# A decoder layer on one core: sums placed apart from their readers in groups of seven, and four more groups of seven in the second gate/up products

## The chip, the cores and the metric

The kernel runs on one core of one Trainium2 chip. The metric is the device time of one execution in microseconds (us). Three runs of the kernel before took 2227.22, 2227.85 and 2228.51 us; the median is 2227.85 us.

## The reference

One decoder layer over 256 tokens of width 2048, in float32: a half feed-forward, a pair of token mixers, a second half feed-forward and a gated embedding, each followed by a layer norm. The change touches the feed-forwards, above all the second one:

```python
def swiglu(x, w_gu, w_down):
    g, u = jnp.split(x @ w_gu, 2, axis=-1)
    return (jax.nn.silu(g) * u) @ w_down
...
        h = layer_norm(alpha * h + 0.5 * swiglu(h, w_ffn1_gu[i], w_ffn1_down[i]), ln_g[i, 0], ln_b[i, 0])
...
        h = layer_norm(alpha * h + 0.5 * swiglu(h, w_ffn2_gu[i], w_ffn2_down[i]), ln_g[i, 2], ln_b[i, 2])
```

Here `x` is 256 x 2048, `w_gu` 2048 x 11264 (gate and up side by side) and `w_down` 5632 x 2048.

## The kernel before

**Products in three parts.** Every float32 number is held as a high part of the type `fp32r` and a low part, the rest. ScalarE (ACT) makes the high part with a cast, VectorE (DVE) the low part with a subtraction (line 107 and line 108). A product then takes three matmuls on TensorE (PE): low x high, high x high, high x low (lines 459 to 461, the method `add` of `Sum`).

**Blocks and units.** The gate/up products run in eleven blocks `j` of 512 gate and 512 up columns; `f2` in a name is the second feed-forward, `f1` the first. The 2048 rows of the weights are cut into eight pairs `p` of 128-row pieces, and each block handles each pair as one unit. The order of the units is a string of letters, one unit each, in `gu_units`:

- `P`, plain: two weight chunks of 512 KB (gate and up) are loaded, and each is made into high and low: two casts on ACT and two subtractions on DVE of 128x1024. PE does 24 matmuls.
- `F`, folded: as `P`, but the low part of the second chunk is made by ACT (the negated copy, line 170) and an accumulating DMA from the POOL queue (line 171), so that DVE has one subtraction less.
- `S`, a group of seven (class `Seven`): the 2x2 block product of two token halves and two column halves is done with seven products in place of eight, 21 matmuls. It needs sums of the weights first: `t1` and `t3` (tile `uf_gu`, lines 256 and 257), `t2` and `t4` (tile `vf_gu`, lines 258 and 259), all on DVE at 128x512. Then four splits follow, each a cast on ACT and a subtraction on DVE: the first chunk (`hf_gu`, `lf_gu`), the block b22 (`bf_gu`, half the size), and the two sums (`huf_gu`, `luf_gu`; `hvf_gu`, `lvf_gu`).
- `D`, prepared (class `Prepared`): a group of seven whose sums were made and written to DRAM during the mixers; it loads them, and only two splits are left.

A block's groups of seven share four PSUM banks (`f22s` for block 2, `f23s` for block 3) beside the four of its gate and up results (`f2g`, `f2u`).

**What sets the order.** The program is recorded by hand: each engine executes its instructions in the order in which the code issues them. `fill` takes units from `plan`, loads them and makes them (the splits and sums) as far ahead of PE as `room` has slots and as the queue is below 45 us of matmul time. So a make stands in DVE's and ACT's streams among the other work of the block: after a block's last group of seven, `seven_common` (lines 578 to 582) takes the shared banks out; after its last unit, lines 1085 to 1087 add the gate and up banks, apply Silu on ACT and multiply. One to five units later a transposed copy of the result is fetched and put together by ACT (`f2a<-mf`, line 226, two copies).

Of the kernel before, what the change touches and what calls it, by code (L numbers as in the profile page):

```python
# [9 lines left out]
F32R = mybir.dt.float32r  # L10
# [3 lines left out]
ALU = mybir.AluOpType  # L14
PSUM = bass.MemoryType.PSUM

P = 128
# [26 lines left out]
SEVEN = (0, 1, 2, 3)  # L44

AHEAD = {1: (4, 5), 2: (4,), 3: (4, 5), 4: (4,), 5: (4, 5), 6: (4,), 7: (4, 5), 8: (4,)}
AHEAD_SLOTS = 36

DELAY = {"f1": 2, "f2": 1}

# [14 lines left out]
def layer(ctx: ExitStack, tc: tile.TileContext, io):  # L65
    nc = tc.nc
    sync, act, dve, pool, pe = nc.sync, nc.scalar, nc.vector, nc.gpsimd, nc.tensor
# [14 lines left out]
    def slot(shape, dt, name):  # L82
        return slots.tile(shape, dt, tag="slot", name=name)
# [22 lines left out]
    def split(dst_hi, dst_lo, src, lo_engine=None):  # L106
        act.copy(dst_hi, src)  # L107
        (lo_engine or dve).tensor_tensor(dst_lo, src, dst_hi, ALU.subtract)  # L108

    class Chunk:  # L110
# [18 lines left out]
        def make(self):  # L129
            self.make_hi()  # L130
            split(self.hi, self.lo, self.raw)
# [71 lines left out]
    class Turn:  # L203
# [7 lines left out]
        def part(self):  # L211
            of_src = self.src.bitcast(U16).rearrange("p a (n h) -> p h a n", h=2)
            self.words = slot([P, 2, self.a, self.b * P], U16, "w" + self.name)
            for h in range(2):
                act.copy(self.words[:, h], of_src[:, h])
# [17 lines left out]
    class Seven:  # L233
# [12 lines left out]
        def make(self):  # L246
            a, b = self.a, self.b
            nm = a.name
            b11, b21, b12, b22 = a.of(a.raw, 0), a.of(a.raw, 1), b.of(b.raw, 0), b.of(b.raw, 1)
            u, v = (slot([P, 2, 512], F32, w + nm) for w in "uv")  # L250

            def shaped(x):
                return x.rearrange("p (g n) -> p g n", g=2) if a.paired else x

            t1, t3, t2, t4 = (shaped(x) for x in (u[:, 0], u[:, 1], v[:, 0], v[:, 1]))
            dve.tensor_tensor(t1, b11, b12, ALU.add)
            dve.tensor_tensor(t3, b12, b22, ALU.add)  # L257
            dve.tensor_tensor(t2, b11, t3, ALU.add)
            dve.tensor_tensor(t4, t2, b21, ALU.add)  # L259

            def parted(name, x):
                hi, lo = (slot([P, 2, 512], F32R, w + name + nm) for w in "hl")
                split(hi, lo, x)
                return [(hi[:, e], lo[:, e]) for e in range(2)]

            a.make()
            self.b11, self.b21 = a.columns(0), a.columns(1)
            both = slot([P, 2, 512], F32R, "b" + nm)
            self.b22 = both[:, 0], both[:, 1]
            split(shaped(both[:, 0]), shaped(both[:, 1]), b22)  # L270
            self.t1, self.t3 = parted("u", u)
            self.t2, self.t4 = parted("v", v)

    put_by_sums = {}

# [108 lines left out]
    def slots_for_weights(n, ahead=45, far=90):  # L384
        room.update(slots=n, ahead=ahead, far=far)
# [177 lines left out]
    def units_of(order, sevens, ahead=()):  # L563

        sevens, ahead = list(sevens), list(ahead)
        plain = [p for p in range(KD // 2) if p not in sevens + ahead]
        of = {"S": sevens, "D": ahead, "P": plain, "F": plain}
        return [(kind, of[kind].pop(0)) for kind in order]
# [397 lines left out]
    def gu_units(name, j):  # L966
        if j == 0:
            return [("P", p) for p in range(KD // 2)]
        if name == "f2" and j in AHEAD:
            plain = "P" if j < 4 else "F"  # L970
            return units_of(*((f"P{plain}SDSDSP", SEVEN[:3]) if j % 2 else (f"P{plain}SSDSSP", SEVEN)), AHEAD[j])
        order = "FFSSFSSP" if name == "f1" or j > 8 else "PFSSFSSP"
        return units_of(order, SEVEN[: order.count("S")])

# [20 lines left out]
    def plan_ffn(name):  # L995
        for j in range(KF // 4):
            block_units(gu_units(name, j), gu_keys(name, j))
        first, second, held = down_units(HELD_PAIRS[name == "f2"])
        block_units(first, down_keys(name, 0))
        block_units(second, down_keys(name, 1))  # L1000
        plan.extend(Single(down_keys(name, 1)(n, p)) for n in range(2) for p in held)

    def ffn(name, i, ht, norm, keep, residual, keepers, away):
# [33 lines left out]
        for j in range(KF // 4):  # L1037
            pg, pu = banks(f"{name}g{j}"), banks(f"{name}u{j}")
            units = gu_units(name, j)
            n_of = {(0, 0): KD, (0, 1): KD, (1, 0): KD, (1, 1): KD}  # L1040
            for kind, p in units:
# [18 lines left out]
            def before(u, j=j, offset=KD // 2 - len(units)):  # L1060
# [14 lines left out]
                if name == "f2" and j and u == 0:  # L1075
                    slots_for_weights(AHEAD_SLOTS - j)
                if j == KF // 4 - 1 and u in (4, 6):
# [895 lines left out]
```

## Time and profile before

| | |
|---|---|
| median of three runs | 2227.85 us |
| span of the profiled execution | 2226.9 us |
| instructions in it | 29164 |
| granted TensorE clock | 0.999 |
| DVE busy | 2006.5 us, 90% |
| ACT busy | 1440.9 us, 65% |
| POOL busy | 51.7 us, 2% |

The profiled execution has no time of its own beside its span; its span is 0.95 us below the median of the runs, which is what lies around the first and last instruction. The page gives the busy time of each engine, the chain of work that ended last, and the costliest groups of instructions; the trace behind it also gives each instruction with its start, its duration and what the engine waited for. In the second gate/up products, blocks 1 to 10 run from 1492.5 to 1896.2 us, about 40.1 us each.

### The profile page before, as it was taken

To read this page: it belongs to the slowest core of one execution; us is meant where nothing else is said; L and a number is where in the kernel's file an instruction comes from. 1 tells how busy PE (TensorE), PEld (TensorE's weight loads), DVE (VectorE), ACT (ScalarE), POOL (GpSimd) and SP (SyncE) were. 2 spreads that over 40 slices of the span, in tenths; PEclk is the share of its full clock that TensorE was granted. 3 is DMA by queue.
4 is the path that set the end of the run, shared out by engine and by line. 5 is a ranking of instruction groups with operands and counts; after the bars stand their busy time and mean duration, and the time that the engine had idled before them with its cause. 6 is when DMAs were issued, how large, how long until landed. Compare 5 with 4: busy or idle time off the path is not lost.

```text
span 2226.9 us, 29164 instructions
## 1 busy us (share of the span) xinstructions
PE 2216.5 (100%) x10137; PEld 1838.3 (83%) x10137; DVE 2006.5 (90%) x2629; ACT 1440.9 (65%) x1680; POOL 51.7 (2%) x66
## 2 busy tenths in 40 slices
PE   9999999999999999999999999999999999999998
PEld 7888888888888888888788888888888888888887
DVE  6999999999988889789999888779999999999977
ACT  6777777776565545557866567466666677765553
POOL 0000000000000000000000000000000000000000
PEclk9999999999999999999999999999999999999999
DMA  9998998978686889846976568888999988777871
GB/s 310 275 251 251 266 271 233 246 228 256 216 301 239 297 281 336 268 172 228 293 232 236 179 205 319 312 302 270 303 297 298 332 240 270 215 237 240 292 283 68
DMA packets 303917, 576.02 MB, mean 259 GB/s; under 512 B 98829, under 2 KB 103821, under 8 KB 303769
## 3 DMA queue, kind: packets, MB, share of 16 engines
q1 hardware_dynamic: 293576, 541.70, 73.4%
q0 software_dynamic: 8208, 29.89, 7.2%
q10 hardware_dynamic: 1984, 2.58, 0.4%
q8 instruction: 79, 1.29, 0.2%
q14 instruction: 70, 0.57, 0.1%
HBM read 490.20 MB, written 33.55 MB: 235 GB/s over the span
## 4 chain that ended last, share of the span: by engine, by line
PE 94%; DVE 2%; DMA 2%; issue 1%; ACT 0%; SPq 0%; ACTq 0%; DVEq 0%; POOLq 0%
PE f1g L461 3%; PE f1g L459 3%; PE f1g L460 3%; PE rqk L410 3%; PE f1u L461 2%; PE f1u L459 2%; PE f1u L460 2%; PE f2g L461 2%; PE f2g L459 2%; PE f2g L460 2%; PE f2u L461 2%; PE f2u L459 2%; PE f2u L460 2%; PE aqk L410 2%; PE f2e L461 1%; PE f2e L460 1%
## 5 line engine op out<-in xcount | busy, mean ns | idle before, releaser
L108 DVE TENSOR_TENSOR lf_gu<-rf_gu,hf_gu 128x1024 fp32r<-128x1024 f32 (+1 forms) x225 | 268.6, 1210 | 24.9 <-ACT hf_gu L107 24.1
L107 ACT CAST hf_gu<-rf_gu 128x1024 fp32r<-128x1024 f32 (+1 forms) x225 | 229.7, 1039 | 24.7 <-DMA rf_gu<-in_f_gu 24.1
L108 DVE TENSOR_TENSOR lw_in_f<-rw_in_f,hw_in_f 128x1024 fp32r<-128x1024 f32 x140 | 167.9, 1219 | 14.0 <-ACT hw_in_f L107 13.6
L108 DVE TENSOR_TENSOR lf_down<-rf_down,hf_down 128x1024 fp32r<-128x1024 f32 x128 | 153.9, 1220 | 17.3 <-ACT hf_down L107 14.5
L107 ACT CAST hf_down<-rf_down 128x1024 fp32r<-128x1024 f32 x128 | 131.5, 1049 | 41.9 <-DMA rf_down<-in_f_down 15.3
L107 ACT CAST huf_gu<-uf_gu 128x1024 fp32r<-128x1024 f32 x76 | 80.1, 1054 | 113.9 <-DVE uf_gu L257 104.1
L107 ACT CAST hw_in_f<-rw_in_f 128x1024 fp32r<-128x1024 f32 x140 | 140.6, 1048 | 5.9 <-DMA rw_in_f<-in_w_in_f 2.9
L107 ACT CAST hvf_gu<-vf_gu 128x1024 fp32r<-128x1024 f32 x76 | 80.2, 1055 | 32.0 <-DVE vf_gu L259 29.8
L108 DVE TENSOR_TENSOR luf_gu<-uf_gu,huf_gu 128x1024 fp32r<-128x1024 f32 x76 | 92.6, 1218 | 0.0
L108 DVE TENSOR_TENSOR lvf_gu<-vf_gu,hvf_gu 128x1024 fp32r<-128x1024 f32 x76 | 92.6, 1218 | 0.0
L459 PE MATMUL f1g<-hf_gu,xt 128*128 128x512 f32 x232 | 90.6, 390 | 1.5 <-ACT hf_gu L107 1.5
L461 PE MATMUL f1g<-lf_gu,xt 128*128 128x512 f32 x232 | 90.4, 389 | 0.0
L460 PE MATMUL f1g<-hf_gu,xt 128*128 128x512 f32 x232 | 90.3, 389 | 0.0
L459 PE MATMUL f2g<-hf_gu,ht 128*128 128x512 f32 x208 | 81.0, 390 | 0.0
L461 PE MATMUL f2g<-lf_gu,ht 128*128 128x512 f32 x208 | 80.9, 389 | 0.0
L460 PE MATMUL f2g<-hf_gu,ht 128*128 128x512 f32 x208 | 80.9, 389 | 0.0
L459 PE MATMUL f1u<-hf_gu,xt 128*128 128x512 f32 x192 | 74.7, 389 | 0.0
L460 PE MATMUL f1u<-hf_gu,xt 128*128 128x512 f32 x192 | 74.7, 389 | 0.0
L461 PE MATMUL f1u<-lf_gu,xt 128*128 128x512 f32 x192 | 74.7, 389 | 0.0
L171 POOL DMA_DIRECT2D lf_gu<-rf_gu x41 | 35.5, 868 | 1637.7 <-PE f2u L461 989.0
L1086 ACT ACTIVATE eve<-eve 128x1024 f32<-128x1024 f32 x20 | 21.2, 1061 | 74.0 <-DVE eve L1085 74.0
L107 ACT CAST huf_down<-uf_down 128x1024 fp32r<-128x1024 f32 x32 | 33.7, 1052 | 49.7 <-DVE uf_down L257 42.4
(1524 smaller groups left out, 6990.8 us busy)
## 6 DMA issues: line engine op xcount, KB each, us to landing
rf_gu<-in_f_gu SPq DMA_DIRECT2D x362, 512.0 KB
rf_down<-in_f_down SPq DMA_DIRECT2D x176, 512.0 KB
rw_in_f<-in_w_in_f SPq DMA_DIRECT2D x148, 512.0 KB
lf_gu<-rf_gu POOLq DMA_DIRECT2D x41, 512.0 KB, 7.9
rw_rv<-in_w_rv SPq DMA_DIRECT2D x32, 512.0 KB
rw_ret<-in_w_ret SPq DMA_DIRECT2D x32, 512.0 KB
rw_mix<-in_w_mix SPq DMA_DIRECT2D x32, 512.0 KB
rw_pg<-in_w_pg SPq DMA_DIRECT2D x32, 512.0 KB
```

Of the source, the lines that this page charges most:

```text
L107: act.copy(dst_hi, src)
L108: (lo_engine or dve).tensor_tensor(dst_lo, src, dst_hi, ALU.subtract)
L171: pool.dma_start(c.lo, c.raw, accum_op=ALU.add)
L410: pe.matmul(ps[f], hi[:, kk, f * P : (f + 1) * P], rhs(k), start=k == 0, stop=k == n_k - 1,)
L459: pe.matmul(o, al, bh, start=first, stop=False)
L460: pe.matmul(o, ah, bh, start=False, stop=False)
L461: pe.matmul(o, ah, bl, start=False, stop=self.left == 0)
L1086: act.activation(g, g, AF.Silu)
```

## The change

`Seven.make` issues its work in another order, with the same 8 operations on DVE and 4 on ACT, and `gu_units` gives other letters to blocks 3, 5, 7 and 9 of the second feed-forward:

| block | before | after |
|---|---|---|
| 3 | PPSDSDSP | PSDSSDSP |
| 5, 7 | PFSDSDSP | PSDSSDSP |
| 9 | FFSSFSSP | FSSFSSSP |

```diff
+SEVEN_MORE = 4
+FIVE = {"f1": (), "f2": (9,)}
@@ class Seven, make
-            dve.tensor_tensor(t1, b11, b12, ALU.add)
-            dve.tensor_tensor(t3, b12, b22, ALU.add)
-            dve.tensor_tensor(t2, b11, t3, ALU.add)
-            dve.tensor_tensor(t4, t2, b21, ALU.add)
-            def parted(name, x):
-                hi, lo = (slot([P, 2, 512], F32R, w + name + nm) for w in "hl")
-                split(hi, lo, x)
-                return [(hi[:, e], lo[:, e]) for e in range(2)]
-            a.make()
-            self.b11, self.b21 = a.columns(0), a.columns(1)
             both = slot([P, 2, 512], F32R, "b" + nm)
             self.b22 = both[:, 0], both[:, 1]
-            split(shaped(both[:, 0]), shaped(both[:, 1]), b22)
-            self.t1, self.t3 = parted("u", u)
-            self.t2, self.t4 = parted("v", v)
+            def part(name):
+                hi, lo = (slot([P, 2, 512], F32R, w + name + nm) for w in "hl")
+                return hi, lo, [(hi[:, e], lo[:, e]) for e in range(2)]
+            dve.tensor_tensor(t3, b12, b22, ALU.add)
+            dve.tensor_tensor(t1, b11, b12, ALU.add)
+            a.make_hi()
+            self.b11, self.b21 = a.columns(0), a.columns(1)
+            act.copy(a.hi, a.raw)
+            act.copy(shaped(both[:, 0]), b22)
+            dve.tensor_tensor(t2, b11, t3, ALU.add)
+            dve.tensor_tensor(a.lo, a.raw, a.hi, ALU.subtract)
+            dve.tensor_tensor(t4, t2, b21, ALU.add)
+            dve.tensor_tensor(shaped(both[:, 1]), b22, shaped(both[:, 0]), ALU.subtract)
+            uh, ul, (self.t1, self.t3) = part("u")
+            act.copy(uh, u)
+            dve.tensor_tensor(ul, u, uh, ALU.subtract)
+            vh, vl, (self.t2, self.t4) = part("v")
+            act.copy(vh, v)
+            dve.tensor_tensor(vl, v, vh, ALU.subtract)
@@ gu_units
+            if j % 2 and j > 1:
+                return units_of("PSDSSDSP", SEVEN, AHEAD[j])
+        if j in FIVE[name]:
+            return units_of("FSSFSSSP", SEVEN + (SEVEN_MORE,))
```

Where two blocks meet, DVE's stream changes most. These are its rows before, at the end of block 2 and the beginning of block 3 (`f22s`, `f2g` and `f2u` are banks of block 2; `_0_6` is the gate chunk of pair 6, `_0_0` that of pair 0, the first group of seven of block 3):

```order
L582 TENSOR_TENSOR evw<-f22s_13857,eve 128x512
L108 TENSOR_TENSOR lf_gu_0_6_14182<-rf_gu_0_6_14125,hf_gu_0_6_14181 128x1024
L108 TENSOR_TENSOR lf_gu_1_6_14210<-rf_gu_1_6_14127,hf_gu_1_6_14209 128x1024
L1085 TENSOR_TENSOR eve<-eve,f2g_13850 128x512
L1085 TENSOR_TENSOR eve<-eve,f2g_13851 128x512
L1085 TENSOR_TENSOR evw<-evw,f2u_13852 128x512
L1085 TENSOR_TENSOR evw<-evw,f2u_13853 128x512
L1087 TENSOR_TENSOR evw<-eve,evw 128x1024
L256 TENSOR_TENSOR uf_gu_0_0_14239<-rf_gu_0_0_14158,rf_gu_1_0_14160 128x512
L257 TENSOR_TENSOR uf_gu_0_0_14239<-rf_gu_1_0_14160 128x512
L258 TENSOR_TENSOR vf_gu_0_0_14240<-rf_gu_0_0_14158,uf_gu_0_0_14239 128x512
L259 TENSOR_TENSOR vf_gu_0_0_14240<-vf_gu_0_0_14240,rf_gu_0_0_14158 128x512
```

And these are the rows of the change at the same place, from the last read of block 2's shared banks on:

```order
L592 TENSOR_TENSOR evw<-f22s_13857,eve 128x512
L267 TENSOR_TENSOR uf_gu_0_0_14189<-rf_gu_1_0_14127 128x512
L268 TENSOR_TENSOR uf_gu_0_0_14189<-rf_gu_0_0_14125,rf_gu_1_0_14127 128x512
L273 TENSOR_TENSOR vf_gu_0_0_14190<-rf_gu_0_0_14125,uf_gu_0_0_14189 128x512
L274 TENSOR_TENSOR lf_gu_0_0_14195<-rf_gu_0_0_14125,hf_gu_0_0_14194 128x1024
L275 TENSOR_TENSOR vf_gu_0_0_14190<-vf_gu_0_0_14190,rf_gu_0_0_14125 128x512
L276 TENSOR_TENSOR bf_gu_0_0_14191<-rf_gu_1_0_14127,bf_gu_0_0_14191 128x512
L279 TENSOR_TENSOR luf_gu_0_0_14203<-uf_gu_0_0_14189,huf_gu_0_0_14202 128x1024
L282 TENSOR_TENSOR lvf_gu_0_0_14207<-vf_gu_0_0_14190,hvf_gu_0_0_14206 128x1024
L1099 TENSOR_TENSOR eve<-eve,f2g_13850 128x512
L1099 TENSOR_TENSOR eve<-eve,f2g_13851 128x512
L1099 TENSOR_TENSOR evw<-evw,f2u_13852 128x512
```

The first group of seven of block 3 is now made ahead of the reading of block 2's gate and up banks (line 1085 before, 1099 now), where it stood behind it; and in its own make the subtraction `lf_gu` now stands between the two sums of `vf_gu`, where the four sums stood side by side.

On PE, block 3 changes at its second unit. Before, plain pair 3 was followed by plain pair 6 (the first row is the last matmul of pair 3):

```order
L461 MATMUL f2u_14221<-lf_gu_1_3_14155,ht_12969 128x512
L459 MATMUL f2u_14222<-hf_gu_1_3_14154,ht_12969 128x512
L460 MATMUL f2u_14222<-hf_gu_1_3_14154,ht_12969 128x512
L461 MATMUL f2u_14222<-lf_gu_1_3_14155,ht_12969 128x512
L459 MATMUL f2g_14219<-hf_gu_0_6_14181,ht_12969 128x512
```

In the change plain pair 6 comes first and the group of seven of pair 0 right behind it:

```order
L471 MATMUL f2u_14239<-lf_gu_1_6_14155,ht_12969 128x512
L469 MATMUL f23s_14240<-hf_gu_0_0_14194,ht_12969 128x512
L470 MATMUL f23s_14240<-hf_gu_0_0_14194,ht_12969 128x512
L471 MATMUL f23s_14240<-lf_gu_0_0_14195,ht_12969 128x512
L469 MATMUL f2g_14236<-hf_gu_0_0_14194,ht_12969 128x512
```

PE reaches the first group of seven of block 3 one plain unit (24 matmuls) earlier than before. In all, PE has 12 matmuls less, DVE 27 subtractions and additions more, ACT eight casts more and three negated copies less, and POOL three accumulating DMAs less. The loads of weights are the same in number and size.

## The prediction

> **What bounds the kernel now.** I read the page first (busy time, chain), then the waits of the second gate/up stage, then single blocks of it in the windows and the timelines.
>
> ```profile
> PE 2216.5 (100%) x10137; PEld 1838.3 (83%) x10137; DVE 2006.5 (90%) x2629; ACT 1440.9 (65%) x1680; POOL 51.7 (2%) x66
> PE 94%; DVE 2%; DMA 2%; issue 1%; ACT 0%; SPq 0%; ACTq 0%; DVEq 0%; POOLq 0%
> ...
> PE f2u L461 <- DMA lf_gu<-rf_gu: 0.8, 1, 0.8
> ```
>
> PE is busy for nearly the whole span and is the chain. In blocks 1 to 10 of the second gate/up stage (1492.5 to 1896.2 us) it waits once, 0.8 us, for the accumulating DMA of a folded unit. A reader who stops here would credit every matmul removed. But DVE stands right behind PE there:
>
> ```profile
> 1572.70:1612.80 40.10, 40.10 (x178) 33.22 (x177) 37.79 (x46) 27.93 (x31) 0.87 (x1) 1.00 0.85 277
> 1612.80:1652.90 40.10, 40.10 (x178) 33.22 (x177) 39.16 (x48) 26.50 (x30) 0.86 (x1) 1.00 0.94 297
> DVE uf_gu L256 <- DMA rf_gu<-in_f_gu: 4.2, 2, 2.5
> DVE lf_gu L108 <- ACT hf_gu L107: 4.0, 10, 0.5
> DVE evw L1085 <- PE f2u L461: 3.1, 4, 1.4
> DVE evw L579 <- ACT eve L578: 1.7, 2, 1.0
> ```
>
> The windows are blocks 3 and 4 (columns: window, length, then busy of PE, PEld, DVE, ACT, POOL). DVE has 37.8 of 40.1 us in an odd block and 39.2 in an even one. The waits are DVE's in the whole stage: 13.0 us in some 404, of which 3.1 are waits for PE, true spare time. How far DVE is ahead is seen in the last group of seven of block 2:
>
> ```profile
> 1556.60 0.69 DVE L256 TENSOR_TENSOR uf_gu<-rf_gu,rf_gu 128x512 f32<-128x512 f32 x1
> 1557.20 0.68 DVE L257 TENSOR_TENSOR uf_gu<-rf_gu 128x512 f32<-128x512 f32 x1
> 1557.99 0.69 DVE L258 TENSOR_TENSOR vf_gu<-rf_gu,uf_gu 128x512 f32<-128x512 f32 x1
> 1558.71 0.69 DVE L259 TENSOR_TENSOR vf_gu<-vf_gu,rf_gu 128x512 f32<-128x512 f32 x1
> 1559.33 1.22 DVE L108 TENSOR_TENSOR lf_gu<-rf_gu,hf_gu 128x1024 fp32r<-128x1024 f32 x1
> 1560.46 0.68 DVE L108 TENSOR_TENSOR bf_gu<-rf_gu,bf_gu 128x512 fp32r<-128x512 f32 x1
> 1561.06 1.22 DVE L108 TENSOR_TENSOR luf_gu<-uf_gu,huf_gu 128x1024 fp32r<-128x1024 f32 x1
> 1562.20 1.22 DVE L108 TENSOR_TENSOR lvf_gu<-vf_gu,hvf_gu 128x1024 fp32r<-128x1024 f32 x1
> 1563.33 1.22 DVE L108 TENSOR_TENSOR lf_gu<-rf_gu,hf_gu 128x1024 fp32r<-128x1024 f32 x1
> 1564.91 2.36 DVE L108 TENSOR_TENSOR lf_gu<-rf_gu,hf_gu 128x1024 fp32r<-128x1024 f32 x2 [0.35 <-ACT hf_gu L107]
> ...
> 1564.09 0.39 PE L460 MATMUL f22s<-hvf_gu,f2fh 128*128 128x512 f32 x1
> 1564.31 0.39 PE L461 MATMUL f22s<-lvf_gu,f2fh 128*128 128x512 f32 x1
> ```
>
> `lvf_gu` is ready at 1562.20 + 1.22 = 1563.42, PE reads it at 1564.31: a lead of 0.9 us. In this stage PE and DVE are two bounds side by side. What DVE gets more than its spare time and this lead, PE has to wait.
>
> **The change part by part.** *Matmuls.* Four units of 24 become four of 21: 12 matmuls less. One starts 0.22 us (1564.31 - 1564.09; 0.227 over longer rows) behind the other, though each is shown with 0.39. That is 12 x 0.227 = 2.7 us less on PE. It is worth that only where DVE keeps up.
>
> *Sums apart from readers.* From start to start a 128x512 operation takes 0.60 us (1557.20 - 1556.60), but `t4`, which reads `t2`, starts 0.72 behind it (1558.71 - 1557.99), and `t2`, which reads the sum before it, 0.79 here. Other groups show 0.72 for both. So 2 x 0.12 = 0.24 us go for each group of seven once no reader stands right behind its sum.
>
> ```profile
> L256 DVE TENSOR_TENSOR uf_gu<-rf_gu,rf_gu 128x512 f32<-128x512 f32 x36 | 24.6, 685 | 4.2 <-DMA rf_gu<-in_f_gu 4.2
> ```
>
> There are 36 groups in these blocks: 36 x 0.24 = 8.6 us less on DVE. Elsewhere the same saving falls where PE has hardly a wait to lose, and I count it nothing.
> [...]
>
> *Four more groups.* A new group takes DVE 4 x 0.60 for the sums, 0.60 for `bf_gu` and 3 x 1.135 (1561.06 to 1562.20 to 1563.33) for the other low parts: 6.41 us. It takes the place of a plain unit in block 3 (2 x 1.135 = 2.27) and of a folded one in blocks 5, 7 and 9 (1.135 each, the rest of its work is ACT's and a DMA's). That is 25.64 - 2.27 - 3.41 = 20.0 us more on DVE. The left-hand forms of pair 4 exist already for the prepared units, so block 9 needs none. ACT gets some 3 us more of casts, hidden in its 12 us of spare time per block. The loads are the same; three accumulating DMAs go.
>
> *The tail on ACT.* `hvf_gu` needs `t4`. Now `t4` stands behind `lf_gu` on DVE:
>
> ```profile
> 1559.49 1.05 ACT L107 CAST hvf_gu<-vf_gu 128x1024 fp32r<-128x1024 f32 x1 [0.47 <-DVE vf_gu L259]
> 1560.45 1.05 ACT L107 CAST hf_gu<-rf_gu 128x1024 fp32r<-128x1024 f32 x1
> 1561.40 2.57 ACT L226 COPY f2a<-mf 128x1024 uint16<-128x1024 uint16 x2
> 1563.84 2.94 ACT L107 CAST hf_gu<-rf_gu 128x1024 fp32r<-128x1024 f32 x3
> ```
>
> Queued behind `hvf_gu` on ACT are a cast, two copies of 2.57 us together and the cast for which DVE waits at 1564.91 (0.35 us). Before, `t4` ends 1559.40 - 1556.60 = 2.80 us behind the group's start. In the new order it ends at 3 x 0.60 + 1.135 + 0.69 = 3.63. ACT's tail begins 0.83 later, and DVE arrives 0.24 earlier: the wait grows by 1.07 us. The ten waits of 4.0 us above are this one, once a block, so DVE loses 10 x 1.07 = 10.7 us. The bounds are 0, if ACT catches up elsewhere (as it does where no copies stand behind a group), and 10 x 1.5 = 15, if the first groups of a block wait too. I take 10.7: same rows, same places.
>
> *PE's turn at block 3, 5, 7, 9.* The first group now comes after one plain unit, 24 x 0.227 = 5.4 us. Its bank, by the order of the program, was a gate bank of the block before, and the reading of it now stands behind the whole make:
>
> ```profile
> 1568.32 0.68 DVE L579 TENSOR_TENSOR evw<-eve,f22s 128x512 f32<-128x512 f32 x1
> 1571.03 2.35 DVE L108 TENSOR_TENSOR lf_gu<-rf_gu,hf_gu 128x1024 fp32r<-128x1024 f32 x2
> 1573.30 1.28 DVE L1085 TENSOR_TENSOR eve<-eve,f2g 128x512 f32<-128x512 f32 x2
> 1583.58 0.39 PE L459 MATMUL f23s<-hf_gu,ht 128*128 128x512 f32 x1
> ```
>
> Today the bank is read at 1573.30 and written at 1583.58. In the change, DVE is at 1571.03 + 6.41 = 1577.4 when it begins to read, done at 1578.1, and PE arrives at 1583.58 - 5.44 = 1578.1. Nothing is left over: any lag of DVE shows here as a wait of PE. This is a place, not a further price, since DVE does the same work.
>
> *Sum.* DVE: 20.0 - 8.6 + 10.7 = 22.1 us more. Against that stand the waits that it can give up: 3.1 for PE surely, 5.9 for DMA (4.2) and for ACT at line 579 (1.7) perhaps. DMAs come at 277 and 297 GB/s in the two windows, with a share of 0.85 and 0.94, so a slower stage leaves them some room; I count a third, 2. With the lead of 0.9: 22.1 - 3.1 - 2 - 0.9 = **16 us slower**. As DVE bounds these blocks then, the 2.7 us of PE and its one wait are not to be had besides. The profiled span of 2226.9 gets 2243; with the 0.95 us between it and the median, 2227.85 + 16 = 2244 us.
>
> **The rivals.**
> 1. *PE stays the bound.* If DVE's lead did suffice, 2.7 us go, and at most the 0.8 of waiting: 2224.3. For it speaks PE at 100%; against it the 0.9 us of lead and the 20 us that come. It decides if DVE's net gain in work is below its 13 us of waits, that is, if the tail term is nought and all waits can be filled. Chance 0.06.
> 2. *The tail does not grow.* 22.1 - 10.7 - 3.1 - 2 - 0.9 = 5.4: 2233. For it: ACT has 12 us spare a block; against it: its four instructions are in a row without idle time in the view. Chance 0.12.
> 3. *The bubbles stay.* By the rows this needs a hold on DVE at every sum, though no reader is next: 16 + 8.6 = 24.6, so 2252.5. [...] Chance 0.05.
> 4. *More waits.* The folded unit that remains inside block 9 has its DMA landing late already:
>
> ```profile
> 1837.93 0.50 PE L461 MATMUL f2u<-lf_gu,ht 128*128 128x512 f32 x1 [0.78 <-DMA lf_gu<-rf_gu]
> ```
>
> It is issued behind ACT's work for the groups ahead of it; PE now reaches it with no lead, so it may cost some 4 us more, and the DMA waits may all remain (2): 16 + 6 = 22, or 2250. Chance 0.07.
>
> That the change does not do what it says is excluded: the rows of the program show the 12 matmuls gone.
>
> **How the numbers follow.** The forecast, 2244, has 0.70. Its own bounds: without the tail's growth in half the blocks and with all waits filled 16 - 5.4 - 3.9 = 7, with the larger tail and no DMA wait filled 16 + 4.3 + 2 = 22: 2235 to 2250. The range goes from 2232 to 2252, so that it takes in rivals 2 and 4; left out are rivals 1 and 3 and the forecast's edges, under 2 in 10. A measurement of this kernel can tell some 0.2%, 4.5 us, from no change. Faster by that would need more than rival 1 gives: 0.02. Within it: the rest of rival 1 and half of rival 2, 0.10. Slower: 0.88.
>
> **What would show it.** In the changed profile: ten waits of `lf_gu` for `hf_gu` of about 1.4 us in place of 0.4; no waits of line 1085's successor for PE; starts of 0.60 us throughout the sums; PE waiting a microsecond or two at the first `f23s`, `f25s`, `f27s` and `f29s`, and for `luf_gu` or `lvf_gu` in the last groups of the even blocks; the folded unit inside block 9 waiting longer than 0.8; a PE as before outside the stage. I am wrong if PE runs through blocks 1 to 10 without such waits, or if the loss arises outside them.

## The result, and the profile after

Four runs of the changed kernel took 2244.1 to 2248.14 us, median 2245.47; the kernel before took 2227.66 beside them. The ratio is 1.0085, with a 95% interval of 1.0073 to 1.0098: slower by some 18 us (17.8 between the medians, 18.9 by the ratio). The profiled span is 2244.2 us, 17.3 longer than before.

The busy times and the chain of the changed kernel's page:

```profile
PE 2220.9 (99%) x10125; PEld 1836.8 (82%) x10125; DVE 2004.4 (89%) x2656; ACT 1442.8 (64%) x1685; POOL 49.2 (2%) x63
PE 92%; DVE 4%; DMA 2%; ACT 1%; issue 1%; SPq 0%; ACTq 0%; DVEq 0%
```

Read by themselves these lines would hide the change: over the whole span DVE is *less* busy than before. In the second gate/up products its busy time rises from 419.2 to 433.1 us; outside them it falls by 16.0, because sums that start 0.60 us apart overlap in the records, where each is shown with some 0.69. What is new is DVE's share of the chain, 4% in place of 2, at PE's cost. The loss is all in the second gate/up products: from 1446.0 to 1913.6 us after, from 1447.0 to 1896.2 before, 18.4 us more. They begin 1.0 us earlier, but that is not shown to be the change's: in e2 and e6, experiments below that keep the old order of the sums, they begin at 1445.7 and 1444.7 us.

The waits of PE in these products (what waited, for what, us in total, times, longest), where before there was one row of 0.8 us:

```profile
PE f2u L471 <- DMA lf_gu<-rf_gu: 6.2, 3, 4.7
PE f27s L469 <- DVE eve L1099: 1.8, 1, 1.8
PE f25s L469 <- DVE eve L1099: 1.8, 1, 1.8
PE f23s L469 <- DVE eve L1099: 1.5, 1, 1.5
PE f29s L469 <- DVE eve L1099: 1.2, 1, 1.2
PE f28s L471 <- DVE luf_gu L279: 0.8, 1, 0.8
PE f26s L471 <- DVE luf_gu L279: 0.7, 1, 0.7
PE f29s L471 <- DVE lf_gu L274: 0.5, 1, 0.5
```

PE waits for DVE at the first group of seven of blocks 3, 5, 7 and 9, in the last groups of the even blocks, and for the folded units in blocks 9 and 10. DVE's own waits in the same stretch:

```profile
DVE lf_gu L112 <- ACT hf_gu L111: 17.0, 11, 2.1
DVE evw L589 <- ACT eve L588: 1.9, 2, 1.0
DVE f2f2l L112 <- ACT f2f2h L111: 1.2, 1, 1.2
DVE lf_gu L274 <- ACT hf_gu L271: 1.1, 1, 1.1
DVE evw L1099 <- PE f2u L471: 0.9, 1, 0.9
```

The waits for DMA (4.2 us before) are gone, those for PE are 0.9 instead of 3.1, and the waits of `lf_gu` for `hf_gu` are 17.0 us instead of 4.0. DVE has become the later of the two engines, and ACT keeps it waiting once a block.

How one late block end runs on into the next block is seen in the timeline between blocks 4 and 5. First DVE (start, duration, line, operation; in brackets the idle time ahead of it):

```profile
1638.84 0.69 DVE L267 TENSOR_TENSOR uf_gu<-rf_gu 128x512 f32<-128x512 f32 x1
1639.44 0.69 DVE L268 TENSOR_TENSOR uf_gu<-rf_gu,rf_gu 128x512 f32<-128x512 f32 x1
1640.04 0.69 DVE L273 TENSOR_TENSOR vf_gu<-rf_gu,uf_gu 128x512 f32<-128x512 f32 x1
...
1641.78 0.69 DVE L275 TENSOR_TENSOR vf_gu<-vf_gu,rf_gu 128x512 f32<-128x512 f32 x1
...
1645.25 1.22 DVE L112 TENSOR_TENSOR lf_gu<-rf_gu,hf_gu 128x1024 fp32r<-128x1024 f32 x1
1647.96 3.50 DVE L112 TENSOR_TENSOR lf_gu<-rf_gu,hf_gu 128x1024 fp32r<-128x1024 f32 x3 [1.49 <-ACT hf_gu L111]
...
1660.50 1.28 DVE L1099 TENSOR_TENSOR eve<-eve,f2g 128x512 f32<-128x512 f32 x2
```

Then ACT beside it, and PE at the end:

```profile
1642.56 1.06 ACT L281 CAST hvf_gu<-vf_gu 128x1024 fp32r<-128x1024 f32 x1 [1.29 <-DVE vf_gu L275]
1643.52 1.04 ACT L111 CAST hf_gu<-rf_gu 128x1024 fp32r<-128x1024 f32 x1
1644.46 2.56 ACT L230 COPY f2a<-mf 128x1024 uint16<-128x1024 uint16 x2
1646.89 2.94 ACT L111 CAST hf_gu<-rf_gu 128x1024 fp32r<-128x1024 f32 x3
...
1661.32 0.47 PE L469 MATMUL f25s<-hf_gu,ht 128*128 128x512 f32 x1 [1.81 <-DVE eve L1099]
```

`t4` (line 275) starts at 1641.78, ACT's `hvf_gu` right behind it, then a cast, the two copies of `f2a` and the cast that DVE needs at 1647.96. From there on DVE hardly pauses (no gap over 0.15 us): three low parts, the reading of the shared banks, a whole group of seven, and at 1660.50 the reading of the gate bank for which PE has been waiting. PE begins `f25s` at 1661.32.

### The profile page after: what moved, and what is told of

It reads as the page before. It is cut to its first block, busy times and chain, and to the rows that moved or that the text cites. A ratio compares the mean times of both kernels' runs of the same rounds, so it can differ in the third digit from the quotient of the medians.

```text
span 2244.2 us, 29126 instructions
## 1 busy us (share of the span) xinstructions
PE 2220.9 (99%) x10125; PEld 1836.8 (82%) x10125; DVE 2004.4 (89%) x2656; ACT 1442.8 (64%) x1685; POOL 49.2 (2%) x63
## 4 chain that ended last, share of the span: by engine, by line
PE 92%; DVE 4%; DMA 2%; ACT 1%; issue 1%; SPq 0%; ACTq 0%; DVEq 0%
PE f1g L471 3%; PE f1g L469 3%; PE f1g L470 3%; PE rqk L420 3%; PE f1u L471 2%; PE f1u L469 2%; PE f1u L470 2%; PE f2g L470 2%; PE f2g L469 2%; PE f2g L471 2%; PE f2u L471 2%; PE aqk L420 2%; PE f2u L469 2%; PE f2u L470 2%; PE f2e L471 1%; PE f2e L469 1%
## 5 line engine op out<-in xcount | busy, mean ns | idle before, releaser
L112 DVE TENSOR_TENSOR lf_gu<-rf_gu,hf_gu 128x1024 fp32r<-128x1024 f32 (+1 forms) x144 | 170.0, 1205 | 50.7 <-ACT hf_gu L111 50.0
L112 DVE TENSOR_TENSOR lw_in_f<-rw_in_f,hw_in_f 128x1024 fp32r<-128x1024 f32 x132 | 158.0, 1218 | 13.0 <-ACT hw_in_f L111 12.8
L111 ACT CAST hf_gu<-rf_gu 128x1024 fp32r<-128x1024 f32 (+1 forms) x144 | 145.5, 1036 | 19.6 <-DMA rf_gu<-in_f_gu 15.7
L111 ACT CAST hw_in_f<-rw_in_f 128x1024 fp32r<-128x1024 f32 x132 | 132.6, 1049 | 7.3 <-DMA rw_in_f<-in_w_in_f 4.4
L112 DVE TENSOR_TENSOR lf_down<-rf_down,hf_down 128x1024 fp32r<-128x1024 f32 x96 | 115.1, 1219 | 21.8 <-ACT hf_down L111 19.4
L111 ACT CAST hf_down<-rf_down 128x1024 fp32r<-128x1024 f32 x96 | 98.7, 1050 | 26.7 <-DMA rf_down<-in_f_down 12.6
L274 DVE TENSOR_TENSOR lf_gu<-rf_gu,hf_gu 128x1024 fp32r<-128x1024 f32 x80 | 97.4, 1218 | 1.1 <-ACT hf_gu L271 1.1
L279 DVE TENSOR_TENSOR luf_gu<-uf_gu,huf_gu 128x1024 fp32r<-128x1024 f32 x80 | 97.4, 1218 | 0.0
L271 ACT CAST hf_gu<-rf_gu 128x1024 fp32r<-128x1024 f32 x80 | 83.6, 1045 | 0.0
L469 PE MATMUL f2g<-hf_gu,ht 128*128 128x512 f32 x196 | 76.4, 390 | 0.0
L470 PE MATMUL f2g<-hf_gu,ht 128*128 128x512 f32 x196 | 76.3, 389 | 0.0
```

Source lines behind the costliest of these rows:

```text
L271: act.copy(a.hi, a.raw)
L274: dve.tensor_tensor(a.lo, a.raw, a.hi, ALU.subtract)
L279: dve.tensor_tensor(ul, u, uh, ALU.subtract)
L469: pe.matmul(o, al, bh, start=first, stop=False)
L470: pe.matmul(o, ah, bh, start=False, stop=False)
```

## The experiments

The theories go by letters. A is the prediction's own account: DVE is the bound of these blocks, and its new work and the longer tail on ACT make the loss. B lets the new order of the sums be a gain by itself, C makes the place of the first group, behind one plain unit, the price, whatever DVE has to do, and D lets the folded unit in block 9 be a loss of its own. Later A is split: in A1 all work on DVE counts, wherever it stands; in A2 only what stands on the chain through ACT at a block's end and on to the bank of the next first group, shown above. The kernel before took 2225.96, 2226.16 and 2225.89 us beside the four groups of runs (2226.16 for two of them). The change itself ran beside 2227.66, so differences from it are taken by the ratios; as each ratio has an interval of 0.1 to 0.3% to either side, such a difference is uncertain by some 4 us.

### The order of the sums alone

e1 is the changed kernel with the units as before:

```diff
-FIVE = {"f1": (), "f2": (9,)}
+FIVE = {"f1": (), "f2": ()}
...
-            if j % 2 and j > 1:
-                return units_of("PSDSSDSP", SEVEN, AHEAD[j])
```

> The new order inside the groups of seven alone, with the units of before. Theory A (DVE and the ACT tail bound the stage): DVE gains 36 x 0.24 = 8.6 us and loses some 10.7 us in the waits of lf_gu for hf_gu, so the two cancel: 2226 to 2230 us, with these waits at some 14 us in blocks 1 to 10 in place of 4.0. Rival B (the order is a pure gain, the units are the whole loss): waits for hf_gu stay near 4 us, time 2225 to 2227. Either way PE has no wait at the first group of a block.

Measured: 2229.65 us, ratio 1.0016 [1.0006, 1.0026]. DVE's largest wait in the blocks, and PE's only one:

```profile
DVE lf_gu L112 <- ACT hf_gu L111: 19.8, 14, 1.7
PE f2u L471 <- DMA lf_gu<-rf_gu: 2.2, 2, 1.5
```

The new order takes 8.6 us of bubbles from DVE and gives 15.8 us of waiting for ACT (19.8 against 4.0). With the old units DVE had spare time for most of that. The order by itself is no gain; it costs some 3.7 us (1.3 to 5.8 by the interval). That is within A's range, with waits for ACT longer than A's 14 us; B, with waits near 4 us, falls.

### The units alone

e2 is the kernel before with the new units:

```diff
+SEVEN_MORE = 4
+FIVE = {"f1": (), "f2": (9,)}
...
+            if j % 2 and j > 1:
+                return units_of("PSDSSDSP", SEVEN, AHEAD[j])
...
+        if j in FIVE[name]:
+            return units_of("FSSFSSSP", SEVEN + (SEVEN_MORE,))
```

> The four more groups alone, with the order of before inside a group. Theory A: DVE has 4 x 6.66 - 5.68 = 21 us more and no longer tail; less the waits that it gives up (5) and the lead (0.9) that is some 13 to 15 us: 2240 to 2243, waits for hf_gu near 4 us. Rival B (the order gains, the units lose): slower than the change as it stands, 2248 to 2254. Rival C (the place of the first group behind one plain unit is the price, whatever DVE has to do): 2245 as the change.

Measured: 2241.79 us, ratio 1.0072 [1.0057, 1.0087]: 15.8 us, the greater part. The tail is short (`lf_gu` waits 5.5 us for `hf_gu`), PE waits all the same, 6.3 us for the folded units and 0.9 at `f25s` and `f27s`. That is within A's range; B is too high, and C's 2245 lies above all four runs. With e1's 3.7 it makes 19.5; the whole change is 17.8 by the medians and 18.9 by the ratio. Within the noise the two parts add up.

### Without block 9, and block 9 alone

e3 is the change with block 9 as before, e4 the new order of the sums with the new units in block 9 alone:

```diff
 e3:
-FIVE = {"f1": (), "f2": (9,)}
+FIVE = {"f1": (), "f2": ()}
 e4:
-            if j % 2 and j > 1:
-                return units_of("PSDSSDSP", SEVEN, AHEAD[j])
```

> The change without its part in block 9. Theory A: DVE has 5.0 us less (6.41 - 1.14 - 0.25), so 11 to 12 us above before: 2238 to 2240; the folded unit inside block 9 still waits, 1 to 2 us, as it comes with no lead. Rival D (the 4.7 us of waiting for the fold of block 9 and the half clock behind it are a loss of their own, apart from DVE): 2236 or less, 7.5 us and the 1.3 at the first group of block 9 below the change.

> The change without its part in blocks 3, 5 and 7. Theory A: DVE has 5.0 + 10.7 - 8.6 = 7 us more in the stage, but blocks 1 to 8 can fill their own waits, so what comes up in block 9 is 4 to 8 us: 2231 to 2236, most of it at the fold inside block 9. Rival D (the fold is late by itself): the wait of some 4.7 us and the half clock as in the change, 2235 to 2237. Rival C: one first group, some 1.5 us, 2229.

Measured: e3 2241.43 us, ratio 1.0070 [1.0055, 1.0085]; e4 2234.2 us, 1.0039 [1.0024, 1.0054]. So block 9 is worth 0.15% (3.3 us, not clear of the noise) on top of the others and 0.23% (5.1 us) on top of e1. e3 came out 1.4 us above A's range, and far above D's 2236; e4 lies within A's range and, in the median, below D's. What A left out is in e3's trace: two stretches of 3.4 us at a granted clock of 0.50, of which the last section tells, make 16 matmuls 0.2 us longer each, 3.2 us. In e3 the waits at the first groups are those of the change (1.6, 1.8 and 1.8 us), and a folded unit still makes PE wait 3.0 us, though block 9 is the old one: it is one of block 10 (at 1891.0 us), while the one inside block 9, for which A expected 1 to 2 us, makes PE wait not at all. In e4 all of PE's 5.7 us are waits for folded units, and none is for a first group. So this wait turns up where DVE and ACT happen to be late; e11 below tests whether it is a loss of its own.

### The copies later

In the change the two copies of `f2a` come one unit behind a block's last one. e5 lets them come three units behind, so that they stand clear of the tail; e6 is the same edit in the kernel before:

```diff
-DELAY = {"f1": 2, "f2": 1}
+DELAY = {"f1": 2, "f2": 3}
```

> The change, with the two copies of the transposed result on ACT (f2a<-mf) two takings of a unit later (the number DELAY of f2 is 3 in place of 1), so that they no longer stand between hvf_gu of a block's last group and the cast for which DVE waits. Nothing else is changed. Theory A: the waits of lf_gu for hf_gu fall from 17 to some 5 us, and the time by as much less what else is late: 2233 to 2238. Rival C (the place of the first group is the price): no change from 2244 to 2246, waits of PE for eve as before.

> Control: the kernel before with the same later copies. Theory A: PE is not kept waiting there, so nothing is gained: 2225 to 2228. If later copies help by themselves: 2222 or less.

Measured: e5 2246.81 us in the median, ratio 1.0084 [1.0054, 1.0113], but its runs spread widely: 2235.28, 2245.38, 2248.24 and 2251.82. e6: 2229.74, ratio 1.0019 [1.0005, 1.0034]; three of its runs took 2225.73 to 2226.79 and three 2232.68 to 2234.34, where 2225 to 2228 was expected. So the edit makes the time unsteady even in the kernel before. The time of e5 missed its range in all runs but the lowest, whose granted clock was 1.000 over the whole run, against 0.995 to 0.997 in the others. DVE's and PE's waits show what became of the gain:

```profile
DVE lf_gu L112 <- ACT hf_gu L111: 1.4, 2, 1.1
PE f2u L471 <- DMA lf_gu<-rf_gu: 12.8, 5, 8.0
```

The tail's waits are down to 1.4 us from 17.0, and with them the waits at `f23s`, `f25s` and `f27s` are gone: PE begins block 9's first group at 1820.7 us in e5 and at 1827.9 in the change, 7.2 us earlier. That much of the mechanism is shown. But part of the waiting for ACT has only moved: DVE's waits at line 589 are 9.4 us in e5, 1.9 in the change. And a new wait comes up behind, 8.0 us for one folded unit of block 10. From issue to landing (shortest, median, longest) the accumulating DMAs between 1800 and 1910 us took in e5, and in the changed kernel behind it:

```profile
DMA to landing us min/median/max: 5.3/9.0/14.9
```

```profile
DMA to landing us min/median/max: 6.7/8.8/9.3
```

The same parameter moves the fetching of the transposed result as well, and the DMA of 14.9 us falls into a stretch (1880 to 1890 us) with its DMA engines fully busy (a share of 1.27 and 1.12 in its two halves) and only 145 and 115 GB/s moved. In e5 a transposed fetch was issued 3.4 us ahead of this DMA; but in the change one was issued 4.3 us ahead of a DMA that landed after 9.3 us, so the cause of the 14.9 stays open. The lesson of e5 is that the tail can't be taken off by moving the copies without paying elsewhere.

### Less work at two places

e7 leaves out two subtractions, `luf_gu` and `lvf_gu`, in the last group of seven of blocks 3, 5, 7 and 9; e8 the same two in the first group of these blocks. PE multiplies by the high part where the low one would stand. That is 4 x 2 x 1.135 = 9.1 us less on DVE in both, and nothing less on PE or ACT:

```diff
+SPARED = [("f2_gu", j, 0, p) for j, p in ((3, 3), (5, 3), (7, 3), (9, 4))]
...
+                if a.key in SPARED:
+                    hi = lo = slot([P, 2, 512], F32R, "h" + name + nm)
...
-            dve.tensor_tensor(ul, u, uh, ALU.subtract)
+            spared = a.key in SPARED
+            if not spared:
+                dve.tensor_tensor(ul, u, uh, ALU.subtract)
...
 e8:
+SPARED = [('f2_gu', 3, 0, 0), ('f2_gu', 5, 0, 0), ('f2_gu', 7, 0, 0), ('f2_gu', 9, 0, 0)]
```

> The change; the last group of seven of blocks 3, 5, 7 and 9 leaves out the low parts of its two sums (luf_gu, lvf_gu) and PE takes the high part in their place, so DVE has 8 x 1.135 = 9.1 us less, and all else is as in the change. Theory A1 (the sum of DVE's work decides, as the prediction counted): 9 us less than the change, 2235 to 2237. Theory A2 (a chain through ACT at the end of each block decides; DVE only arrives earlier at its wait for hf_gu): 2243 to 2246, and the waits for hf_gu longer by what is left out, some 2 us in each of these blocks.

> The same left out in the first group of seven of blocks 3, 5, 7 and 9, which stands behind the chain and ahead of the reading of the gate banks. A1: as e7, 2235 to 2237. A2: here the 2.27 us of each block count, 2234 to 2238, and the waits of PE for eve at the first groups go.

Measured: e7 2246.14 us, ratio 1.0090 [1.0075, 1.0105]; e8 2236.3, 1.0046 [1.0031, 1.0061]. Rows of DVE and PE in e7:

```profile
DVE lf_gu L114 <- ACT hf_gu L113: 25.0, 16, 2.2
PE f27s L480 <- DVE eve L1110: 1.8, 1, 1.8
```

And in e8:

```profile
DVE lf_gu L114 <- ACT hf_gu L113: 17.5, 12, 2.1
PE f2u L482 <- DMA lf_gu<-rf_gu: 4.7, 1, 4.7
```

In e7 9.1 us of work became 8.0 us of waiting (25.0 against 17.0), and PE's waits stayed: the same work on DVE is worth nothing ahead of ACT's tail. In e8 it stands behind the tail and ahead of the bank that PE needs, and there it is worth 0.39%, 8.7 us; the waits of `f23s` to `f29s` for the reading of the gate bank (line 1099 in the change) are gone. A1 falls, A2 stands. So does C fall: PE comes to the first groups at the same place in e8, yet the waits there are gone, and nearly half of the price with them.

### The first two sums exchanged

In e9 the make is t3, t1, t2, t4 and then the two low parts, with the units of the change: `t2` no longer reads the sum right ahead of it, `t4` still does, and it ends 0.12 us earlier than before the change. e10 is the same make with the old units. The edit, from the change to e9:

```diff
             dve.tensor_tensor(t2, b11, t3, ALU.add)
-            dve.tensor_tensor(a.lo, a.raw, a.hi, ALU.subtract)
             dve.tensor_tensor(t4, t2, b21, ALU.add)
+            dve.tensor_tensor(a.lo, a.raw, a.hi, ALU.subtract)
```

> The units of the change; the make in the order t3, t1, t2, t4, then the two low parts (as before, but with the first two sums exchanged, so that t2 no longer reads the sum right before it; t4 still reads t2). t4 ends 0.12 us earlier than before the change behind a group's start, and ACT's tail (hvf_gu, hf_gu, two copies, hf_gu) with it. Theory A2 (the chain through ACT at a block's end counts): the 13 us that the waits of lf_gu for hf_gu grew by in the changed kernel are gone (4 us or less over ten waits), the 20 us of new work on DVE stay, the first half of the bubbles goes: 8 to 13 us over before, 2234 to 2239. Rival (the tail costs nothing, the new units alone make the loss, as the old make with the new units gave 2241.8): within 3 us of that, 2239 to 2245, with the same waits at the first groups.

> The kernel before, with the first two sums of a group exchanged (t3, t1, t2, t4) and nothing else. Theory A2: t2 no longer waits for DVE's own t3, 0.12 us less for each of some 36 groups in the stage, 4 us of DVE's time, but PE has 0.8 us of waits to give up there: 2225 to 2227, within 0.1% of before. Rival (bubbles on DVE reach the time): 2220 to 2223.

Measured: e9 2238.15 us, ratio 1.0051 [1.0038, 1.0065]; e10 2226.14 us, 0.9998 [0.9989, 1.0007]. In e9 (DVE's row first, then PE's) the tail is nearly back to its old size, and the waits at the first groups are half as long (`f27s` as `f25s`):

```profile
DVE lf_gu L112 <- ACT hf_gu L111: 6.1, 10, 2.2
PE f25s L469 <- DVE eve L1099: 0.8, 1, 0.8
```

Between the change and e9 lie 0.34%, 7.6 us. By the prediction's sizes it would be 10.7 of tail less 36 x 0.12 = 4.3 of bubbles, 6.4. Against e2 (2241.79), whose make differs from e9's by the first exchange alone, the gain is 3.6 us for 4.3 of bubbles; by the ratios it is 0.21%, hardly clear of the noise. A part of both differences can be the clock: e9's trace has no stretch at 0.50 in these products (its windows from 1825 to 1890 us have 1.00 throughout), the change's has one that costs 2.4 us and e2's one that costs 1.6. In e10 the same 4.3 us are worth nothing that the runs can tell (0.02 us; the interval goes from -2.4 to 1.6). Some 2.6 us of it can be found in the trace; DVE's wait for PE was 3.1 us before, and now it is this row and two more of 0.8 and 0.3:

```profile
DVE evw L1097 <- PE f2u L471: 4.6, 4, 1.4
```

With the old units PE is the bound, DVE finishes earlier and waits for PE: that is shown. With the new ones DVE is the bound, and the saving seems to arrive; its size is not settled by these runs.

### The folded unit of block 9 made plain

```diff
-            return units_of("FSSFSSSP", SEVEN + (SEVEN_MORE,))
+            return units_of("FSSPSSSP", SEVEN + (SEVEN_MORE,))
```

> The change with the folded unit in the middle of block 9 made plain (its accumulating DMA goes, DVE gets a low part of 1.1 us more). Theory A2 (the wait of 4.7 us for that DMA shows DVE's and ACT's lateness at the place where PE meets it): the wait goes, and the half clock behind it, but PE then waits for lvf_gu or lf_gu in the last groups of block 9 or at block 10 instead; 1 to 4 us less than the change, 2241.5 to 2244.5. Rival (the fold and the half clock behind it are a loss of their own): 7 us less, 2238 to 2239.

Measured: 2246.73 us, ratio 1.0096 [1.0081, 1.0111]: no gain over the change at all, so the rival falls, and A2's range was too low by 2 us. PE's waits in e11:

```profile
PE f2u L471 <- DMA lf_gu<-rf_gu: 3.7, 3, 2.9
PE f29s L471 <- DVE lf_gu L274: 2.2, 3, 1.1
...
PE f29s L471 <- DVE luf_gu L279: 1.4, 1, 1.4
```

The wait of 4.7 us is gone; in its place `f29s` waits for `lf_gu` three times and once for `luf_gu`, because DVE has a low part more to make; in the second gate/up products PE's waits add up to 15.2 us in e11 and to 15.0 in the change. The long wait for the DMA was where PE met DVE's and ACT's lateness in block 9, not a loss beside it. The half clock did not go with it, as the last section shows.

### Prepared units ahead of the first groups

e12 has the make of e9 and block 9 as before. It also has another order of units in blocks 3, 5 and 7, which the expectation doesn't name: a prepared unit stands ahead of the first group of seven. Two edits, then, not one:

```diff
-FIVE = {"f1": (), "f2": (9,)}
+FIVE = {"f1": (), "f2": ()}
...
-                return units_of("PSDSSDSP", SEVEN, AHEAD[j])
+                return units_of("PDSSDSSP", SEVEN, AHEAD[j])
```

> The kernel of e9 (units of the change in blocks 3, 5 and 7; make t3, t1, t2, t4, two low parts) with block 9 as before. Three new groups on DVE in place of four. Theory A2 (only DVE work on the chain counts): e9's 12 us less the share of block 9, which was 4.0 us in the changed kernel and 4.6 alone: 7 to 9 us over before, 2233 to 2235.5; waits of PE at the first groups 0.8 us or less. It does not beat before. Rival (block 9's loss was the new order's alone, since there its fold and half clock made it): no gain against e9, 2237 to 2239.

Measured: 2229.78 us, ratio 1.0015 [1.0006, 1.0025], 3.9 us over before and below the range. PE's largest waits (`f25s` has one like that of `f27s`):

```profile
PE f2u L471 <- DMA lf_gu<-rf_gu: 0.9, 1, 0.9
PE f27s L471 <- DVE luf_gu L279: 0.8, 1, 0.8
```

PE comes to the first group one unit later than in e9 and finds its bank free. How much of the gain against e9 is this and how much is block 9 can't be told from the one run. What it does tell: with three new groups, the short tail and PE's turn put off, the loss is down to 3.9 us, and 9 matmuls less still buy nothing. No version beat the kernel before; e10 is level with it.

## Why the prediction was right

The forecast of 2244 with 2232 to 2252 holds the 2245.47, and the cause it named is the one found: DVE stood right behind PE, and was given more than its spare time and lead. Its places came true too: the long `lf_gu` waits, the sums 0.60 us apart (1640.04 - 1639.44), the first groups, the last groups of the even blocks, the fold in block 9. One sign came only in part: DVE still waits for PE once, 0.9 us.

*Its sum, term by term.* DVE's books in the stage, with what the rows show:

| term | predicted | measured |
|---|---|---|
| four new groups | +20.0 | +20.0 (6.41 us for one make: 1645.25 - 1638.84) |
| bubbles | -8.6 | -8.6 (0.60 for `t2`, none behind `t4`) |
| waits for ACT's tail | +10.7 | +13.0 (17.0 - 4.0) |
| `lf_gu` of a group for `hf_gu` | none | +1.1 |
| waits at line 579, now 589 | 0, or given up in part | +0.2 (1.9 - 1.7) |
| waits for PE given up | -3.1 | -2.2 (3.1 - 0.9) |
| waits for DMA given up | -2 (with those of line 579) | -4.2 |
| lead | -0.9 | not measured (the estimate, -0.9) |
| sum | 16 | 18.4 |

The stage is 18.4 us longer, and 1.0 less ahead of it makes the span's 17.3, within rounding. That the books close proves little by itself: an engine's work and waits add up to the length of a stage whichever engine bounds it. They show where the time went; that DVE's work makes the price is shown by e8 against e7, and that it made none before by e10. The tail was 1.55 us a wait (17.0 over 11), not 1.4; in the slower stage the waits for the weights' DMAs went whole (4.2 us), where a third of 5.9 was counted. These two errors of 2 us nearly cancel, which is luck; what is left of the 2.4 us between 16 and 18.4 are the waits of 1.1 and 0.2 that the sum did not have and the 0.9 of waiting for PE that stayed. `t4` ends 1641.78 + 0.69 - 1638.84 = 3.63 us behind its group's start, as worked out.

*The step that was too simple* is "DVE: new work less waits", with all work counted alike. The books above don't say what a microsecond of work is worth: e7's 9.1 us were worth nothing, e8's 8.7. Between ACT's tail and the next block's first group each microsecond counts; ahead of the tail DVE only waits longer. That the plain sum came out right rests on the new groups making the blocks' first groups urgent, which the prediction named as a place and "not a further price". In that respect the good sum is in part luck. It also has no term for PE at half clock, 2.4 us of matmul time in block 9; what that is worth in the kernel's time no run shows.

*The bubbles.* They are real on DVE, 0.72 against 0.60 us from start to start for sums that are shown with some 0.69. With DVE as the bound, crediting them fits what was measured (3.6 us for half of them between e2 and e9, hardly clear of the noise); where PE is the bound they are worth nothing (e10). In the 36 groups of these blocks before, `t2` starts 0.72 to 0.79 us behind the sum that it reads and `t4` 0.72 or 0.73 behind `t2`; in the 40 of the change `t2`, which no longer reads the sum right ahead of it, starts 0.60 behind that one. So in these rows a sum that has to wait for the one right ahead starts 0.12 us or more later than one that has not; what takes this time is not shown.

*The rivals.* PE did not stay the bound (rival 1): one wait of 0.8 us became eleven kinds, 15.0 us in all. The tail did grow (rival 2), 13.0 us. The bubbles went (rival 3). Of rival 4 the wait came, the price didn't: the fold in block 9 cost 4.7 us in place of 0.8, with more behind it, yet e11 without it is no faster.

PE's side agrees. By the timeline its starts fall behind the pace of 0.227 us by 7.2 us at the four first groups, 4.0 in the other groups of blocks 3 to 8, 9.0 in the rest of block 9 and 1.5 in block 10: 21.7, less some 1.2 that were there before and 2.7 for the 12 matmuls, about 18.

## What to carry to other kernels

Where two engines run side by side at nearly full load, taking work from one and giving it to the other moves the bound (here the new units alone, with 2.7 us of matmuls less on PE, cost 15.8 us: e2); compare the lead of the second, read at a single operand (0.9 us here), with what it is given, before counting what the first saves. A dependent operation put later in an in-order stream delays all that stands behind its reader on the *other* engine (here `t4` ends 0.83 us later in its group, and with the old units DVE's waits for ACT grew from 4.0 to 19.8 us: e1), so follow that queue to its end before breaking up a chain of sums. And ask of each microsecond on which side of the next wait it lies: the same 9.1 us of work were worth 0 and 8.7.

## What the runs showed of the hardware

*PE at half clock after waits.* The wait for the folded unit in block 9 costs more than its 4.7 us. Windows of the changed kernel around it (busy of PE, PEld, DVE, ACT, POOL, then the granted clock, the DMA share, GB/s):

```profile
1846.00:1848.50 2.50, 1.88 (x5) 1.49 (x6) 2.50 (x4) 1.05 (x1) 0.00 (x0) 0.50 0.38 147
1848.50:1852.00 3.50, 3.50 (x10) 2.73 (x9) 3.50 (x5) 2.41 (x3) 0.00 (x0) 0.50 0.00 0
1852.00:1856.00 4.00, 4.00 (x19) 3.28 (x18) 4.00 (x7) 1.15 (x2) 0.00 (x0) 1.00 0.22 60
```

And PE's timeline there:

```profile
1846.62 0.79 PE L471 MATMUL f2u<-lf_gu,ht 128*128 128x512 f32 x1 [4.72 <-DMA lf_gu<-rf_gu]
1847.22 0.63 PE L469 MATMUL f2u<-hf_gu,ht 128*128 128x512 f32 x1
1847.64 0.63 PE L470 MATMUL f2u<-hf_gu,ht 128*128 128x512 f32 x1
```

For some 5 us the matmuls start 0.42 us apart (1847.64 - 1847.22) instead of 0.227, at a granted clock of 0.50: about a dozen matmuls at 0.2 us each, 2.4 us more. The stretch at 0.50 goes from 1845.2 to 1852.0 us, so it begins while PE still waits. In e4 a wait of 3.51 us has the same behind it: starts 0.42 us apart (1837.79 - 1837.37), and a granted clock of 0.66 from 1835 to 1840 us. In e3 the wait of 3.0 us that ends at 1891.0 is followed by 3.4 us at 0.50 (its windows, same columns):

```profile
1888.82:1892.23 3.41, 1.20 (x5) 1.03 (x6) 3.41 (x6) 1.04 (x1) 0.00 (x0) 1.00 0.95 377
1892.23:1895.65 3.42, 3.42 (x9) 2.66 (x9) 3.04 (x4) 3.17 (x3) 0.00 (x0) 0.50 0.17 42
```

PE was busy for 1.20 of the 3.41 us ahead of this stretch. In e3 the wait of 1.8 us at `f27s` is followed by half clock too (matmuls behind it are shown with 0.63 us in place of 0.39); in the change the same wait, 1.81 us, is not (granted clock 1.00 from 1743 to 1752 us), nor is a wait of 3.0 us in e2 (1.00 from 1840 to 1850 us).

e11 shows it with short waits (its windows, same columns):

```profile
1855.00:1858.50 3.50, 1.25 (x4) 0.77 (x5) 3.50 (x5) 2.24 (x4) 0.00 (x0) 0.88 0.78 249
1858.50:1861.00 2.50, 2.50 (x7) 1.88 (x7) 1.93 (x2) 2.50 (x3) 0.00 (x0) 0.50 0.86 288
```

Here no single wait is longer than 1.4 us. Two of them, 1.07 and 1.4 us, leave PE busy for 1.25 of 3.50 us, and behind them the granted clock is 0.50 too. So in e11 two short waits close together had behind them what a long one had in the change. How long a wait is does not by itself tell whether half clock follows: 1.8 us had it in e3, 3.0 us in e2 did not. What decides it is not shown by these runs.

*A transposed fetch that was only moved* (e5) went with an accumulating DMA of 512 KB landing after 14.9 us, where those of the change in the same stretch took at most 9.3, and the time of the kernel varied by 16 us from run to run; that the one made the other is not shown.
